# Low parts of selected weight blocks, query-decay products and norm sums issued on VectorE instead of GpSimd

## The chip, the cores and the metric

The kernel runs on one core of a Trainium2 chip. The metric is the device time of one execution in microseconds (us); the time before is the median of three runs. The core has TensorE (matmuls; PE in the profile, its weight loads PEld), VectorE (DVE), ScalarE (ACT), GpSimd (POOL) and the DMA queue of SyncE (SP). Every engine takes its own instructions in the order in which they were put in its queue.

## The reference

One inference step of a two-layer streaming encoder in float32, on 1024 frames of a new stream and 64 frames of a running one; the model width is 1024. Both layers are `x += mixer(rmsnorm(x)); x += conv_ffn(rmsnorm(x))`, and a last RMSNorm follows.

- Layer 0's mixer is multi-scale causal pooling: the mean over a window of 2, 4, 8 or 16 frames less the frame itself, then a 256x256 matrix per group of channels.
- Layer 1's mixer is a gated linear recurrence with 8 heads of dimension 128: `proj = h @ w_in` gives queries, decays f, values and output gates; inside a chunk the products of queries and keys are weighted by the products of the decays between them; a 128x128 state is carried from chunk to chunk; then a norm per head, the gate and `w_out`.
- The ConvFFN is `up = h @ w_up` (2 x 2816 columns), a causal convolution over 3 frames on the gate half, `silu(conv) * val`, and `@ w_down`.

```
def rmsnorm(x, g):    return x * rsqrt(mean(x * x) + EPS) * g
def conv_ffn(h, ...): gate, val = split(h @ w_up); hid = silu(conv3(gate)) * val; return hid @ w_down
```

## The kernel before, in words

Activations lie with the channels on the 128 partitions, 8 tiles of channels, and the 1088 frames in three chunks c of 384, 384 and 320 columns. Each matrix product is made of three TensorE passes in a reduced float32 format (`mm3`, lines 180 to 182): high part of the weight by high part of the data, high by low, low by high. A value a is split into `hi`, a rounding copy on ScalarE, and `lo = a - hi`, a subtraction: `split` (lines 184 to 186) does that for activations and `load_ready` (lines 109 to 130) for weights.

Weights are fetched in blocks of 128x512 by SP into five raw buffers. `load_ready` works a hand-written list (`q_unit`, `q_mix`): as soon as one of 8 slots (12 in the recurrence) is free, the block's `hi` goes to ScalarE (line 128) and its `lo` to GpSimd (line 129). The slot is freed by `drop` when the last matmul with the block has been issued. The list has in this order: the pooling matrices `pw` (4 blocks), layer 0's ConvFFN, the recurrence (phase "g": 64 blocks of `in`, 16 of `out`), layer 1's ConvFFN. In a ConvFFN, j counts 22 tiles of up-projected columns in 11 groups of two. The first group and the last chunk of all groups use plain products (parts a11 to a22 of `up`, which are quarters of the matrix); the other groups use a scheme with seven instead of eight products, whose weights are sums of two raw blocks (made on VectorE, line 152) and whose data are sums of activations (`sums`, lines 423 to 456, on VectorE, made once per layer after the norm). Key `("up", l, j, part)` is such a block, `("upp", ...)` a plain block of the last group, `("dn", l, j, half)` a block of `w_down`.

The RMSNorm (`norm`, lines 353 to 422) has a kind: 0 before layer 0's ConvFFN, 1 before the recurrence, 2 before layer 1's ConvFFN, 3 at the end. It squares the 8 tiles on ScalarE (lines 362 and 365), adds them up in two chains of three additions (line 366: even d and odd d), adds the two (line 373), transposes on TensorE (line 378), makes 1/sqrt in 11 small steps on VectorE (`rstd`, lines 333 to 344), transposes back (line 391), multiplies (line 417) and splits (line 185 `hi`, line 186 `lo`).

The recurrence runs per head h and chunk c: `proj` (queries, decays and so on on TensorE, lines 828 to 867), `core` (lines 870 to 1039), and after two heads `outp`. In `core` line 915 makes `qq = q * f`; then come three levels, and in each VectorE multiplies queries and keys by products of decays (line 936), TensorE makes the scores (line 945, `pl`), and VectorE puts them in place under masks (line 960). A fourth level (lines 969 to 978) and the state follow. Two heads' projections and cores overlap.

The order of TensorE's instructions is written out by the kernel itself (`Task`, `run`): every step gives its own length and the lag until the next step of its task may start, in constants such as `LAT_LEVEL` and `N_RSTD`; the plan does not change with the engine that makes a `lo`. The order on the other engines is set by the compiler's scheduler. VectorE, ScalarE and GpSimd work through their queues in order, so an instruction that waits holds up what is behind it.

Called "turns" here are the stretches in which one stage ends and the next begins: pooling into layer 0's ConvFFN, that into the recurrence, the recurrence into layer 1's ConvFFN.

Of the kernel before, what the change touches and what calls it, by code (L numbers as in the profile page):

```python
# [9 lines left out]
F32 = mybir.dt.float32  # L10
# [4 lines left out]
ALU = mybir.AluOpType  # L15
# [50 lines left out]
def trunk_kernel(ctx: ExitStack, tc: tile.TileContext, xtok, xs_tok, hist_tok, xf, par, gmix, pw, winm, ident_in,  # L66
                 masks_in, w_up, w_dn, w_in, w_out, s0, y_out, npool, nhg, nconv):
    nc = tc.nc
# [30 lines left out]
    def bankB(nm):  # L99
        return pB.tile([P, 512], F32, name=nm, tag="B")  # L100
# [5 lines left out]
    free = [(i, False) for i in range(NR)]  # L106
    extra_w = []

    def load_ready(most=None):

        while queue and (most is None or len(loaded) < most):
            ph, key, make = queue[0]
            own = [p for p in free if p[1]] if ph == "g" and key[:2] not in (("out", H - 2), ("out", H - 1)) else []
            p = own[0] if own else next((p for p in free if not p[1]), None)
            if p is None:
                return
            free.remove(p)
            queue.pop(0)
            places[key] = p
            i, extra = p  # L120
            nm = "_".join(str(k) for k in key)
            if extra:
                hi, lo = (extra_w[i // 2][:, (i % 2 * 2 + b) * HW_:(i % 2 * 2 + b + 1) * HW_] for b in range(2))
            else:
                hi = wp.tile([P, HW_], F32R, name=f"whi{nm}", tag=f"whi{i}", bufs=1)
                lo = wp.tile([P, HW_], F32R, name=f"wlo{nm}", tag=f"wlo{i}", bufs=1)
            src = make(nm)
            nc.scalar.copy(hi, src)  # L128
            nc.gpsimd.tensor_tensor(lo, src, hi.bitcast(F32), op=ALU.subtract)  # L129
            loaded[key] = (hi, lo)  # L130

    def raw_block(nm, src, i):
# [51 lines left out]
    def split(hi, lo, src, lo_eng):  # L184
        nc.scalar.copy(hi, src)  # L185
        lo_eng.tensor_tensor(lo, src, hi.bitcast(F32), op=ALU.subtract)  # L186
# [114 lines left out]
    hn_hi = [hnp.tile([P, ND, NCOL[c]], F32R, name=f"hnhi{c}") for c in range(3)]  # L301
    hn_lo = [hnp.tile([P, ND, NCOL[c]], F32R, name=f"hnlo{c}") for c in range(3)]
# [11 lines left out]
    def piece(what, tag, i, dt):  # L314

        if held.get(tag, (None,))[0] != what:
            held[tag] = what, room(f"{what}{tag}", tag, None, dt)
        return held[tag][1][:, i * NMAX:(i + 1) * NMAX]

    def row(l, c, d):  # L320
        return piece(f"row{l}", *ROWS[c][d], F32)

    def slot(nm, tag, bufs=1, dt=F32, w=SLOT):
        return wk.tile([P, w], dt, name=nm, tag=tag, bufs=bufs)

    def col(base, i):
        return prm[:, base + i:base + i + 1]

    def rstd(ss, nb, nm):

        t = tiny.tile([P, 3, 4], F32, name=f"nt_{nm}", tag="newton")
        m, y, a = (t[:, i, :nb] for i in range(3))
        nc.vector.tensor_scalar(m, ss[0], 1.0 / ss[1], EPS, op0=ALU.mult, op1=ALU.add)
        nc.vector.tensor_scalar(a.bitcast(I32), m.bitcast(I32), 1, None, op0=ALU.logical_shift_right)
        nc.vector.tensor_scalar(y.bitcast(I32), a.bitcast(I32), -1, 0x5F1FFFF9, op0=ALU.mult, op1=ALU.add)

        nc.vector.scalar_tensor_tensor(a, y, -0.703952253, y, op0=ALU.mult, op1=ALU.mult)
        nc.vector.tensor_tensor(a, a, m, op=ALU.mult)
        nc.vector.scalar_tensor_tensor(y, a, 1.68191408, y, op0=ALU.add, op1=ALU.mult)
        nc.vector.tensor_tensor(a, y, y, op=ALU.mult)  # L340
        nc.vector.tensor_tensor(a, a, m, op=ALU.mult)
        nc.vector.tensor_scalar(m, a, 0.375, -1.25, op0=ALU.mult, op1=ALU.add)
        nc.vector.tensor_tensor(a, a, m, op=ALU.mult)
        nc.vector.scalar_tensor_tensor(y, a, 1.875, y, op0=ALU.add, op1=ALU.mult)
        return y

    def blocks(c):
        n = NCOL[c]
        return [(b * P, min(P, n - b * P)) for b in range((n + P - 1) // P)]
# [3 lines left out]
    def norm(c, gbase, nm, kind):  # L353

        final = kind == 3
        n = NCOL[c]
        tags = ("ge", 3, "cv", 3) if kind == 2 else ("e", 2, "v", 2)
        acc = [slot(f"acc{i}_{nm}", *tags[:2]) for i in range(2)]
        for d in range(ND):
            a = acc[d % 2][:, :n]  # L360
            if d < 2:
                nc.scalar.activation(a, x[c][:, d, :], AF.Square)
            else:
                sq = slot(f"sq_{nm}{d}", *tags[2:])
                last = nc.scalar.activation(sq[:, :n], x[c][:, d, :], AF.Square)
                (nc.vector if kind == 0 or final and c == 2 or d % 2 else nc.gpsimd).tensor_tensor(a, a, sq[:, :n], op=ALU.add)
        if final:
            with tc.issue_after(last.ins):
                for d in range(ND):
                    nc.scalar.activation(x[c][:, d, :], x[c][:, d, :], AF.Copy, scale=col(gbase, d))  # L370
        yield 0.0, N_SUM[kind] + N_LATER[0] * (kind == 1 and c > 0)
        a0, acc = acc
        nc.vector.tensor_tensor(acc[:, :n], acc[:, :n], a0[:, :n], op=ALU.add)
        acc = acc[:, :n]
        pt = bankB(f"nps_{nm}")
        blk = blocks(c)
        for i, (o, w) in enumerate(blk):
            nc.tensor.transpose(pt[:w, i * P:(i + 1) * P], acc[:, o:o + w], ident)
        ss = tiny.tile([P, 4], F32, name=f"ss_{nm}", tag="ss")
        full = sum(1 for _, w in blk if w == P)  # L380
        if full < len(blk):
            nc.vector.memset(ss[:, :len(blk)], 1.0)
        nc.vector.tensor_reduce(ss[:, :full], pt[:, :full * P].rearrange("p (b f) -> p b f", f=P), axis=AX.X, op=ALU.add)
        for i, (o, w) in enumerate(blk):
            if w < P:
                nc.vector.tensor_reduce(ss[:w, i:i + 1], pt[:w, i * P:(i + 1) * P], axis=AX.X, op=ALU.add)
        r = rstd((ss[:, :len(blk)], D), len(blk), nm)
        yield 0.11 * len(blk), N_RSTD[kind] + N_LATER[1] * (kind == 1 and c > 0)
        pr = bankB(f"nr_{nm}")
        for i, (o, w) in enumerate(blk):  # L390
            nc.tensor.transpose(pr[:, o:o + w], r[:w, i:i + 1].to_broadcast([w, P]), ident[:w, :w])
        if kind == 0 and c == 1:
            yield 0.0, L_ROWS
        if kind == 0 and c == 0:
            nc.scalar.copy(piece("r0", *T1[6 + c], F32), pr[:, :n])
        if final:
            rs = slot(f"r_{nm}", "cv", 3)
            nc.scalar.copy(rs[:, :n], pr[:, :n])
        while kind == 2 and c < 2 and not last_proj:
            yield 0.0, 0.2  # L400
        for d in range(ND):
            if final:
                on_pool = c < 2 or d in (2, 5)
                eng, r_ = (nc.gpsimd, rs) if on_pool else (nc.vector, pr)
                eng.tensor_tensor(x[c][:, d, :], x[c][:, d, :], r_[:, :n], op=ALU.mult)

                if c < 2 and d % 2 or c == 2 and (d % 2 == 0 or d == ND - 1):
                    d0 = d - (0 < d and (c < 2 or d % 2 == 0))
                    nc.sync.dma_start(y_out[c][:, d0:d + 1, :], x[c][:, d0:d + 1, :])
            else:  # L410
                if kind == 2 and c < 2 or kind == 0 and c == 1:
                    t = row(kind // 2, c, d)
                elif kind == 0 and c < 2:
                    t = slot(f"hn_{nm}{d}", ("hh1", "hl1")[d % 2], 2, F32, NMAX)
                else:
                    t = slot(f"hn_{nm}{d}", "cv", 3)
                last = nc.vector.scalar_tensor_tensor(t[:, :n], x[c][:, d, :], col(gbase, d), pr[:, :n], op0=ALU.mult, op1=ALU.mult)
                split(hn_hi[c][:, d, :], hn_lo[c][:, d, :], t[:, :n], (nc.vector, nc.gpsimd)[d % 2 and kind == 1])
                if d < ND - 1:
                    yield 0.0, N_STEP[kind]  # L420
        return last.ins
# [61 lines left out]
    def token_sums(c):  # L483
# [38 lines left out]
        if c == 0:  # L522
            load_ready(6)
# [346 lines left out]
    def core(h, c, pr, stage):  # L870

        qt, kk, f = (pr[i] for i in ("q", "k", "f"))
        n = NCOL[c]
# [38 lines left out]


        qq, q = qt[:, :n], qt[:, NMAX:NMAX + n]
        nc.gpsimd.tensor_tensor(qq, q, f[:, :n], op=ALU.mult)
        p0 = prod(kk, q, f"pl{nm}_d")
        nc.vector.tensor_tensor(at[:, :so].rearrange("p (b t) -> p b t", t=P), p0[:, :so].rearrange("p (b t) -> p b t", t=P),
                                ident.unsqueeze(1).to_broadcast([P, full, P]), op=ALU.mult)
# [6 lines left out]
        for lev in range(3):  # L925
# [26 lines left out]
            for i, ps in enumerate(pls):  # L952
                r, num = blk[2 * i][1], min(2, nb - 2 * i)
                dst = at[:r, 2 * i * P:2 * i * P + num * r].rearrange("p (b m w) -> p b m w", b=num, w=4 * hh)
                src = ps[:r, :num * 3 * r // 2].rearrange("p (b e m w) -> p b e m w", b=num, e=2, w=3 * hh)
# [224 lines left out]
```

## Time and profile before

| | us |
|---|---|
| median of 3 runs (2372.25 to 2373.45) | 2372.37 |
| the profiled execution | 2377.06 |
| its span, first to last instruction | 2375.2 |
| TensorE busy | 2284.7 (96%) |
| VectorE busy | 1613.8 (68%) |
| GpSimd busy | 1003.0 (42%) |
| ScalarE busy | 904.3 (38%) |
| granted TensorE clock, mean | 0.981 |

The span is the time from the first to the last instruction of the profiled execution. "Busy" is the union of an engine's instructions; 38111 instructions were recorded, 13830 of them matmuls. The granted clock is a share of TensorE's full rate of 2.4 GHz; at its lower level it runs at 1.2 GHz, and that level shows as 0.5.

### The profile page before, as it was taken

What the parts mean: (1) busy time and instruction counts of PE and PEld (TensorE: products, weight loads), DVE (VectorE), ACT (ScalarE), POOL (GpSimd) and SP (SyncE); (2) the same over time, 40 slices, a digit from 0 to 9 for tenths busy, and PEclk for the clock granted to TensorE, in tenths of its full rate; (3) what the DMA queues carried; (4) which work ended last, traced back from release to release, by engine and by line L of the source; (5) the groups of instructions that cost most, each with busy time, mean ns of one, the idle gap of its engine ahead of it and who ended that gap; (6) DMA issues with size and microseconds to landing.
All of it is one profiled execution on the core that took longest, in us unless ns stands there. A gap on an engine that the chain in (4) does not pass through costs nothing. (4 is left out here: it accounts for less than half of the span.)

```text
span 2375.2 us, 38111 instructions
## 1 busy us (share of the span) xinstructions
PE 2284.7 (96%) x13830; PEld 2231.3 (94%) x13830; DVE 1613.8 (68%) x3728; ACT 904.3 (38%) x1965; POOL 1003.0 (42%) x1054
## 2 busy tenths in 40 slices
PE   9889999999999989999999999889999999999996
PEld 8889999999999989999999999878999999999996
DVE  6786656566666688767667767778766666666567
ACT  5444333334433353323323322345333333443335
POOL 1155554556655562112112211224454555564555
PEclk8999999999999999999999999989999999999998
DMA  7123333333433321001011000102343334433431
GB/s 233 49 81 116 125 121 120 123 125 129 138 116 125 124 69 36 26 18 54 26 35 40 32 26 22 36 25 76 111 130 116 125 119 134 134 124 117 129 120 76
DMA packets 118099, 218.70 MB, mean 92 GB/s; under 512 B 13436, under 2 KB 17404, under 8 KB 117528
## 3 DMA queue, kind: packets, MB, share of 16 engines
q1 hardware_dynamic: 117822, 216.15, 28.0%
q8 instruction: 109, 1.79, 0.3%
q14 instruction: 78, 0.64, 0.1%
q10 hardware_dynamic: 90, 0.12, 0.0%
HBM read 210.51 MB, written 5.72 MB: 91 GB/s over the span
## 5 line engine op out<-in xcount | busy, mean ns | idle before, releaser
L129 POOL TENSOR_TENSOR wloup_a<-rawup_a,whiup_a 128x512 fp32r<-128x512 f32 x368 | 513.1, 1411 | 568.1 <-ACT whiup_a L128 534.4
L128 ACT CAST whiup_a<-rawup_a 128x512 fp32r<-128x512 f32 x368 | 224.2, 617 | 573.8 <-PE dn L181 397.4
L152 DVE TENSOR_TENSOR rawup_a<-rawup_a,rawup_a 128x512 f32<-128x512 f32 x200 | 186.6, 933 | 286.4 <-DMA rawup_a<-w_up_in 261.4
L180 PE MATMUL dn<-hh,whidn 128*128 128x384 f32 (+1 forms) x1056 | 351.5, 333 | 11.5 <-DVE x L757 8.0
L181 PE MATMUL dn<-hl,whidn 128*128 128x384 f32 (+1 forms) x1056 | 348.7, 330 | 0.7 <-DVE hl L186 0.7
L182 PE MATMUL dn<-hh,wlodn 128*128 128x384 f32 (+1 forms) x1056 | 348.9, 330 | 0.0
L757 DVE TENSOR_TENSOR x<-x,dn 128x384 f32<-128x384 f32 (+1 forms) x528 | 262.3, 528 | 97.1 <-PE dn L182 95.5
L180 PEld LDWEIGHTS dn<-hh,whidn 128*128 128x128 f32 x1056 | 200.2, 190 | 18.0 <-DVE x L757 13.4
L181 PEld LDWEIGHTS dn<-hl,whidn 128*128 128x128 f32 x1056 | 200.1, 190 | 1.3 <-DVE hl L186 1.3
L182 PEld LDWEIGHTS dn<-hh,wlodn 128*128 128x128 f32 x1056 | 200.1, 189 | 0.0
L180 PE MATMUL pj<-hnhi,whiin 128*128 128x384 f32 (+1 forms) x528 | 185.0, 350 | 1.1 <-ACT hnhi L185 1.1
L181 PE MATMUL pj<-hnlo,whiin 128*128 128x384 f32 (+1 forms) x528 | 173.0, 328 | 2.4 <-POOL hnlo L186 2.4
L182 PE MATMUL pj<-hnhi,wloin 128*128 128x384 f32 (+1 forms) x528 | 173.2, 328 | 0.0
L630 DVE SCALAR_TENSOR_TENSOR cv<-ge,prm,cv 128x322 f32<-128x322 f32 (+1 forms) x132 | 132.1, 1002 | 48.2 <-ACT cv L629 42.0
L129 POOL TENSOR_TENSOR wlodn<-rawdn,whidn 128x512 fp32r<-128x512 f32 x88 | 119.0, 1354 | 100.9 <-ACT whidn L128 76.8
L960 DVE COPY_PREDICATED at<-masks,pl 128x64 f32<-128x64 uint8 (+7 forms) x432 | 117.0, 293 | 50.5 <-PE pl L945 48.8
L632 ACT ACTIVATE cv<-cv 128x322 f32<-128x322 f32 (+1 forms) x132 | 67.2, 509 | 161.3 <-DVE cv L631 160.9
L180 PE MATMUL pv<-hnhi,whiup_a 128*128 128x320 f32 (+1 forms) x384 | 122.1, 318 | 0.0
L180 PE MATMUL pg<-hnhi,whiup_a 128*128 128x320 f32 (+1 forms) x384 | 122.1, 318 | 0.0
L182 PE MATMUL pg<-hnhi,wloup_a 128*128 128x320 f32 (+1 forms) x384 | 121.7, 317 | 0.0
L182 PE MATMUL pv<-hnhi,wloup_a 128*128 128x320 f32 (+1 forms) x384 | 121.5, 317 | 0.0
L181 PE MATMUL pg<-hnlo,whiup_a 128*128 128x320 f32 (+1 forms) x384 | 121.5, 316 | 0.0
(1234 smaller groups left out, 6199.0 us busy)
## 6 DMA issues: line engine op xcount, KB each, us to landing
rawup_a<-w_up_in SPq DMA_DIRECT2D x568, 256.0 KB, 2.8
rawdn<-w_dn_in SPq DMA_DIRECT2D x88, 256.0 KB, 3.1
rawin<-w_in_in SPq DMA_DIRECT2D x64, 256.0 KB, 2.6
rawupp_a<-w_up_in SPq DMA_DIRECT2D x16, 256.0 KB, 2.7
rawout<-w_out_in SPq DMA_DIRECT2D x16, 256.0 KB, 2.7
xt<-xtok_in SPq DMA_DIRECT2D x7, 448.0 KB, 6.7
x<-xf_in SPq DMA_DIRECT2D x2, 1536.0 KB, 8.7
y_out<-x SPq DMA_DIRECT2D x8, 384.0 KB, 2.3
```

Source lines behind the costliest of these rows:

```text
L128: nc.scalar.copy(hi, src)
L129: nc.gpsimd.tensor_tensor(lo, src, hi.bitcast(F32), op=ALU.subtract)
L152: nc.vector.tensor_tensor(t[0], t[0], t[1], op=bs[2])
L180: nc.tensor.matmul(ps, w[0][:, wsl], a_hi, start=first, stop=False, skip_group_check=more)
L181: nc.tensor.matmul(ps, w[0][:, wsl], a_lo, start=False, stop=False, skip_group_check=more)
L182: nc.tensor.matmul(ps, w[1][:, wsl], a_hi, start=False, stop=last, skip_group_check=more)
L630: nc.vector.scalar_tensor_tensor(t[:, :wd], ge[:, 0:wd], prm[:, cw[0]:cw[0] + 1], t[:, :wd], op0=ALU.mult, op1=ALU.add)
L632: nc.scalar.activation(t[:, :wd], t[:, :wd], AF.Silu)
L757: nc.vector.tensor_tensor(x[c][:, d, :], x[c][:, d, :], pd[:, :n], op=ALU.add)
L960: nc.vector.copy_predicated(dst[:, :, :, d * hh:], mk, a)
```

## The change

The `lo` of a weight block is made on VectorE for all blocks of the recurrence, for `pw`, for `up` with j below 4 and for `dn` with j below 2 of both layers; all other blocks stay on GpSimd. By the list these are 4 `pw`, 80 blocks of the recurrence, and 30 for each layer (8 plain blocks for j = 0 and 1, 9 each for j = 2 and 3, 4 of `dn`): 144. In `norm`, the additions of even d move from GpSimd to VectorE for kinds 1 and 2 (kind 0 had them there, kind 3 is as before). The `lo` of odd d in kind 1 moves to VectorE. In `core` the product `qq` moves to VectorE (24 instructions). What is computed, the transfers, TensorE's and ScalarE's instructions stay as they are.

```diff
+    def lo_engine(ph, key):
+        return nc.vector if ph == "g" or key[0] == "pw" or key[0] in ("up", "dn") and key[2] < (4, 2)[key[0] == "dn"] else nc.gpsimd
...
             nc.scalar.copy(hi, src)
-            nc.gpsimd.tensor_tensor(lo, src, hi.bitcast(F32), op=ALU.subtract)
+            lo_engine(ph, key).tensor_tensor(lo, src, hi.bitcast(F32), op=ALU.subtract)
...
-                (nc.vector if kind == 0 or final and c == 2 or d % 2 else nc.gpsimd).tensor_tensor(a, a, sq[:, :n], op=ALU.add)
+                (nc.vector if kind < 3 or c == 2 or d % 2 else nc.gpsimd).tensor_tensor(a, a, sq[:, :n], op=ALU.add)
...
-                split(hn_hi[c][:, d, :], hn_lo[c][:, d, :], t[:, :n], (nc.vector, nc.gpsimd)[d % 2 and kind == 1])
+                split(hn_hi[c][:, d, :], hn_lo[c][:, d, :], t[:, :n], nc.vector)
...
-        nc.gpsimd.tensor_tensor(qq, q, f[:, :n], op=ALU.mult)
+        nc.vector.tensor_tensor(qq, q, f[:, :n], op=ALU.mult)
```

## Rows read from the trace of the kernel before

**Rows 1.** The page, its first lines: span, and busy time of each engine.
```profile
span 2375.2 us, 38111 instructions
...
PE 2284.7 (96%) x13830; PEld 2231.3 (94%) x13830; DVE 1613.8 (68%) x3728; ACT 904.3 (38%) x1965; POOL 1003.0 (42%) x1054
```

**Rows 2.** Busy time by stretch; after the engines the granted clock, DMA share, GB/s.
```profile
0.00:126.00 126.00, 111.22 (x690) 107.88 (x691) 90.08 (x237) 64.80 (x133) 18.06 (x28) 0.89 0.42 133
126.00:170.00 44.00, 38.60 (x240) 37.44 (x239) 40.80 (x66) 22.90 (x49) 31.42 (x26) 1.00 0.27 86
170.00:836.00 666.00, 659.16 (x3960) 655.31 (x3959) 424.49 (x674) 252.61 (x492) 361.68 (x386) 1.00 0.38 124
836.00:895.00 59.00, 49.55 (x276) 47.06 (x275) 52.30 (x114) 31.44 (x64) 37.69 (x33) 0.91 0.18 60
...
945.00:1515.00 570.00, 562.92 (x3550) 538.07 (x3549) 389.47 (x1456) 169.84 (x485) 103.08 (x102) 1.00 0.10 32
1515.00:1592.00 77.00, 61.08 (x315) 55.54 (x314) 58.85 (x174) 31.27 (x75) 15.25 (x16) 0.82 0.06 19
1592.00:1670.00 78.00, 71.15 (x413) 67.98 (x412) 66.07 (x118) 34.36 (x72) 33.75 (x39) 0.96 0.25 82
```

**Rows 3.** Waits of PE in 0:126, 836:895, 1515:1592: us in total, times, longest.
```profile
PE nps_f L378 <- DVE acc_f L373: 6.1, 2, 3.9
...
PE pj L181 <- POOL hnlo L186: 2.4, 1, 2.4
...
PE pl L945 <- DVE q__16127 L936: 7.3, 2, 3.9
```

**Rows 4.** Timeline near 1091 us, POOL, DVE and PE: start, length, instruction.
```profile
1091.00 1.26 POOL L129 TENSOR_TENSOR wloin<-rawin,whiin 128x512 fp32r<-128x512 f32 x1 [9.78 <-ACT whiin L128]
...
1091.08 1.29 DVE L936 TENSOR_TENSOR q__11445<-q__11445,tp 128x96 f32<-128x96 f32 x1
...
1092.52 0.40 PE L945 MATMUL pl<-q__11445,k__11634 128*128 128x192 f32 x1 [1.35 <-DVE q__11445 L936]
```

**Rows 5.** Timeline near 1026 us, DVE and PE: a level of the recurrence.
```profile
1025.98 0.24 DVE L936 TENSOR_TENSOR q__10771<-q__10771,tp 128x80 f32<-128x80 f32 x1
...
1027.15 0.33 PE L945 MATMUL pl<-q__10771,k__10842 128*128 128x192 f32 x1
```

**Rows 6.** Timeline of DVE near 1646 us, with GpSimd idle.
```profile
1645.60 0.68 DVE L152 TENSOR_TENSOR rawup_a<-rawup_a,rawup_a 128x512 f32<-128x512 f32 x1
1646.20 0.55 DVE L186 TENSOR_TENSOR mix1w<-sum,mix1w 128x384 fp32r<-128x384 f32 x1
```

**Rows 7.** Instructions of line 129 alone by stretch: POOL's busy time (count), granted clock.
```profile
836.00:895.00 59.00, 18.34 (x13) 0.91 0.18 60
945.00:1515.00 570.00, 78.86 (x61) 1.00 0.10 32
...
1620.00:1645.00 25.00, 12.75 (x8) 0.88 0.26 85
```

**Rows 8.** Groups of DVE in 1620:1642: count, busy us, mean ns of one.
```profile
L186 DVE TENSOR_TENSOR hnlo<-sum,hnhi 128x384 fp32r<-128x384 f32 x7 | 7.0, 1014 | 0.0
L437 DVE TENSOR_TENSOR sum<-row1w 128x384 f32<-128x384 f32 x6 | 4.2, 732 | 0.0
L631 DVE SCALAR_TENSOR_TENSOR cv<-ge,prm,cv 128x322 f32<-128x322 f32 x2 | 2.1, 1059 | 0.0
L437 DVE TENSOR_TENSOR sum<-row1w,row1f 128x384 f32<-128x384 f32 x1 | 1.6, 1641 | 0.0
L437 DVE TENSOR_TENSOR sum<-row1q,row1w 128x384 f32<-128x384 f32 x1 | 1.6, 1614 | 0.0
```

**Rows 9.** Timeline of DVE in 1524:1531: three steps of a 1/sqrt.
```profile
1524.84 0.88 DVE L337 SCALAR_TENSOR_TENSOR nt_g<-nt_g 128x3 f32<-128x3 f32 x1
1525.76 0.16 DVE L338 TENSOR_TENSOR nt_g<-nt_g 128x3 f32<-128x3 f32 x1
...
1529.45 1.22 DVE L342 TENSOR_SCALAR nt_g<-nt_g 128x3 f32<-128x3 f32 x1
```

## Prediction, made before the change was run

> **What bounds the kernel now.** I read the page first: TensorE is busy for 2284.7 of 2375.2 us [rows 1]. The change leaves its instructions alone, so it can give back only idle time of TensorE, 90.5 us in all, and what TensorE loses where its clock is halved. The second view, busy time by stretch, says where that is [rows 2]. In 170:836, the body of the first ConvFFN, TensorE idles for 6.8 us of 666; nothing is to be had there, though GpSimd is busy for 361.68 us. The turns are different. Idle of TensorE: 14.8 us in 0:126, 5.4 in 126:170, 9.4 in 836:895, 15.9 in 1515:1592, 6.9 in 1592:1670; the recurrence, 945:1515, has 7.1. In three of these the granted clock is under 1: 0.91, 0.82 and 0.96, worth 0.09 x 59 + 0.18 x 77 + 0.04 x 78 = 22.3 us of full rate. VectorE is nearly full in the turns (40.80 of 44, 52.30 of 59, 66.07 of 78 us) and at 68% in the recurrence (389.47 of 570).
>
> The third view, who TensorE waits for, names VectorE nearly everywhere and GpSimd once: a norm's sum, 6.1 us in the first stretch; the low part of a normalised tile on GpSimd, 2.4 us at the turn into the recurrence; the factor products of the last core, 7.3 us [rows 3]. So VectorE's speed in the turns is the question, and the fourth view shows what slows it: at 1091.08 a product of 96 columns takes 1.29 us, and it ends with a weight's low part that GpSimd began at 1091.00; TensorE has by then waited 1.35 us [rows 4]. A product of 80 columns with GpSimd idle takes 0.24 us [rows 5]. A VectorE instruction with two SBUF inputs is therefore held by GpSimd's to its end, about 1.05 us here. Rows 5 also show the reserve of a level of the recurrence: the product ends at 1026.22, TensorE uses it at 1027.15, 0.93 us later.
>
> **Prices.** A low part on VectorE: no subtraction of that shape is there, but line 152 adds two 128x512 tiles in SBUF in 0.68 us, and its successor starts 0.60 us after it [rows 6]; I take 0.60, with 0.68 as the upper end. The 128x384 operations (norm additions, low parts of tiles, qq) are like line 186 in the same rows: 0.55 us, 0.47 where they stand back to back, by the same 0.08 of overlap. On GpSimd a weight's low part costs 78.86 / 61 = 1.29 us in the recurrence and 12.75 / 8 = 1.59 in a turn [rows 7]. VectorE gets 144 x 0.60 = 86 us, 18 norm additions, 12 low parts and 24 qq at 0.47 = 25 us: 111 us on an engine that idles for 2375.2 - 1613.8 = 761. The sum alone decides nothing; each stretch does.
>
> **Turn into layer 0 (0:126), +1.** Freeing the four `pw` blocks loads four `up` blocks just ahead of the norm sum for which TensorE waits [rows 3]: up to 4 x 0.60 = 2.4 us more in front of it. Two earlier pairs of low parts may hold VectorE less than before, by 4 x (1.05 - 0.60). Ends -1.8 and +2.4; I take +1.
>
> **Second halves of both ConvFFN turns (126:170 and 1592:1670), -2.7 each.** In 1620:1642 VectorE works without a gap on `sums`, and GpSimd makes 8 low parts [rows 7], all of j under 4 or of `dn` under 2, so all move. What the port takes from VectorE there is the excess over an undisturbed length (0.55 us for 384 columns, some 0.54 for the convolution): 7 x 0.46 + 6 x 0.18 + 2 x 0.52 + 1.09 + 1.06 = 7.5 us [rows 8]. Their own work is 8 x 0.60 = 4.8. VectorE is done 2.7 us sooner, and TensorE, which waits for its results, idles for 6.9 us in this turn, so the gain gets through. Layer 0 has the same sequence with 40.80 of 44 us busy and 5.4 us of idle [rows 2]; I take the same. Ends for each: the idle, -5.4 and -6.9, and 0.
>
> Here a rule speaks against the change. The Trainium skill (Trace analysis, Optimizing Scalar/DVE Operations) says that work may be taken off a saturated VectorE, to GpSimd even, and adds that between these two it might not help, since they share a read port. By its first half 4.8 us would be lost in each of these turns; by the rows the port takes 7.5 us.
>
> **Turn into the recurrence (836:895), -2.4.** To VectorE go 12 low parts (the 13th of [rows 7] is of the last group and stays), 8 low parts of tiles and 9 norm additions: 7.2 + 3.8 + 4.2 = 15.2 us, where VectorE has 6.7 us of idle and GpSimd's 37.69 us of holding go away almost wholly. I take these as even, since the blocked time there is spread over many small steps. What is left is the wait of 2.4 us for a tile's low part, which stands in GpSimd's queue behind weights at 1.4 us each (18.34 / 13); on VectorE it takes 0.55. Ends: all the idle, -9.4, and the work that finds no idle, 15.2 - 6.7 = +8.5.
>
> **Recurrence (945:1515), -1.5.** 61 low parts [rows 7] and 21 qq: 36.6 + 9.9 us of new work beside 180 us of idle. A low part now waits in VectorE's queue for ScalarE's high part, with the factor products (line 936) and the masks (line 960) behind it, and TensorE's scores wait for those. Where it is in front it holds the chain 0.60 us, not 1.05; a wait such as that of 1.35 us becomes 0.90. A third of 7.1 us is 2.4; I keep 1.5, as some levels have less reserve than 0.93. Ends -7.1 and the first rival's price.
>
> **Turn out of the recurrence (1515:1592), -1.7.** In 1524:1531 five of the eleven steps of a 1/sqrt take 0.88 to 1.22 us, the first and last of which are shown, instead of 0.16 [rows 9]: between 5 x 0.72 = 3.6 and 5 x 1.06 = 5.3 us more; I take 4.3. Behind them stand the products for which TensorE waits 7.3 us in two waits [rows 3]. GpSimd holds them with three norm additions and two low parts, whose own work is 3 x 0.47 + 2 x 0.60 = 2.6. Ends -7.3 and +2.6.
>
> **Clock, -3.** Parts two, three and five give back 6.8 of 32.2 us of idle in the three stretches with a lowered clock, 21%; of 22.3 us that is 4.7. A stretch at 1.2 GHz that ends in a wait gives nothing back, so 3. Ends 0 and -12.
>
> **The rest at nothing.** SP issues a transfer when a raw buffer is freed, which the low part does; a shorter one frees it earlier, and in the bodies, where GpSimd keeps its blocks, the transfers hide under TensorE. ScalarE's squares in the norms wait for VectorE's additions instead of GpSimd's. What covers a late low part is that a block is loaded when a slot is freed and used only after the blocks ahead of it in the list; without that cover TensorE would wait those 0.60 us, or a pair's 1.20, for every such block.
>
> Sum: +1 - 2.7 - 2.7 - 2.4 - 1.5 - 1.7 - 3 = -13.0. The profiled execution took 2377.06 us, 1.9 more than its span, and would take 2364; the median stands 4.7 us below it, at 2372.37, and goes to **2359.4**.
>
> **Rivals.** (1) *The recurrence's VectorE chain becomes late, slower.* `drop` frees both halves of a matrix at once, so low parts come in pairs in some 30 levels. A pair is 1.20 us, and if it waits 0.6 for ScalarE (one such operation's length), 1.80 against a reserve of 0.93: 0.87 x 30 = 26 us more, 14.6 after the 11.5 of the other parts, 2387. It decides from about 13 late levels on (11.5 / 0.87). For it: rows 5 show little reserve, and queues are in order. Against: VectorE idles for a third of the stage, and holds of 1.05 us go. Chance 0.12.
> (2) *A full engine gets fuller, slower:* the blocks' own work adds, and little comes back, since GpSimd's remaining operations hold VectorE as before. +2.4 + 4.8 + 4.8 + 2.6 - 2.4 - 1.5 = +10.7: 2383. The first half of the Trainium skill's rule above (Trace analysis, Optimizing Scalar/DVE Operations) would have it so. Against it stands the excess in [rows 8]. Chance 0.05.
> (3) *The port's time comes back as own work:* only the 2.4 us of GpSimd's late tile goes, the first turn's +1 stays: 2371. For it: 111 us are added, and work and holds are near each other in every part. Chance 0.15.
> (4) *The waits fall under what halves the clock:* half of the 22.3 us returns, and the turn out of the recurrence gives its whole 7.3: -10 - 11 - 5.6 = 2346. Against: most waits shrink by a third only. Chance 0.18.
> That the moves aren't made is excluded: each is a named engine in the diff.
>
> **Numbers.** Forecast 0.50, its own range 2350 to 2367. What a measurement can tell from no change is 0.2%, 4.7 us. Faster by more: forecast and rival 4, 0.68; within: rival 3, 0.15; slower: rivals 1 and 2, 0.17. The range takes in rivals 3 and 4 and some of the lesser loss: 2344 to 2377.
>
> **What would show it.** In the trace after: the step at 1.29 us [rows 4] back near 0.25, GpSimd nearly idle in the recurrence; line 129 on VectorE at 0.6 to 0.7 us; PE's wait for GpSimd's tile gone; the 1/sqrt steps near 0.16 in the turn out of the recurrence and its wait of 7.3 us at 5 to 6; idle in 1592:1670 some 4 us. Wrong it would be if waits for line 936 in 945:1515 grew beyond 7 us, if line 129 on VectorE showed long waits for ScalarE, or if the turns kept their idle with VectorE's own work in the place of the holds.

## The result, and the profile after

The changed kernel takes 2341.64 us (median of four runs, 2340.37 to 2346.42) against 2372.85 for the kernel before beside it: a ratio of 0.987, 95% interval 0.9856 to 0.9884, that is 31.2 us less. Forecast were 13.0 less, to 2359.4, in a range from 2344 to 2377: the direction and the cause were right, the forecast gain was less than half of the measured one, and the time lies 2.4 us under the range. The fourth rival, 2346, came nearest.

The first lines of the page after, span and busy time of each engine:

```profile
span 2339.5 us, 38021 instructions
...
PE 2269.2 (97%) x13830; PEld 2219.9 (95%) x13830; DVE 1621.5 (69%) x3926; ACT 904.5 (39%) x1965; POOL 755.1 (32%) x856
```

The profiled execution of the changed kernel took 2341.33 us. Beside [rows 1] the span is 35.7 us shorter (4.5 more than the medians differ by; the execution that was profiled before lay 4.7 above its median). Two things make up the 35.7. TensorE idles 70.3 us instead of 90.5, 20.2 less. And it is busy for 15.5 us less with the same 13830 matmuls; its mean granted clock rose from 0.981 to 0.988, so fewer of them ran at the lower level. The forecast held 10.0 us for idle time and 3 for the clock. VectorE took on 198 instructions and is busy for only 7.7 us more: the holds that went were nearly as long as the work that came.

Busy time by stretch after, with borders at the same matmuls as in [rows 2]; the columns are as there:

```profile
0.00:117.70 117.70, 103.91 (x690) 99.74 (x691) 92.19 (x249) 64.72 (x133) 2.90 (x16) 0.97 0.45 143
117.70:158.10 40.40, 37.73 (x240) 37.41 (x239) 39.27 (x79) 23.68 (x50) 13.81 (x13) 1.00 0.32 98
158.10:823.30 665.20, 659.00 (x3960) 655.33 (x3959) 426.11 (x684) 252.45 (x491) 348.29 (x376) 1.00 0.39 124
823.30:881.00 57.70, 48.76 (x276) 47.34 (x275) 53.14 (x143) 30.61 (x64) 2.10 (x3) 0.91 0.19 61
931.00:1494.40 563.40, 562.47 (x3550) 538.07 (x3549) 395.10 (x1541) 170.19 (x485) 2.02 (x20) 1.00 0.10 32
1494.40:1561.20 66.80, 55.78 (x315) 51.21 (x314) 55.96 (x181) 31.31 (x77) 0.38 (x3) 0.90 0.06 19
1561.20:1635.60 74.40, 71.16 (x412) 68.33 (x411) 63.23 (x139) 34.21 (x72) 8.52 (x20) 0.95 0.28 89
```

Both kernels issue the same matmuls in the same order, so the time at which each comes can be compared. The stretches gave back, in us, by the borders of [rows 2]: the first 8.4; 126:170 3.6, and 2.3 more up to 200; the body of layer 0 took back 1.4; 836:895 1.3 (3.6 up to 861 us, of which 2.3 went again behind it); the recurrence 6.6; 1515:1592 10.3; 1592:1670 3.5, and 0.7 up to 1700; after that 0.7. In the recurrence TensorE's idle time fell from 7.1 to 0.9 us.

The same level of the recurrence as in [rows 4], on DVE and PE, some 14 us earlier in the span (line 132 is the low part, line 939 the factor products, line 948 the scores):

```profile
1077.29 0.26 DVE L939 TENSOR_TENSOR q__11445<-q__11445,tp 128x96 f32<-128x96 f32 x1
...
1077.60 0.71 DVE L132 TENSOR_TENSOR wloin<-rawin,whiin 128x512 fp32r<-128x512 f32 x1
...
1077.70 1.05 PE L948 MATMUL pl<-q__11445,k__11634 128*128 128x192 f32 x5 [0.31 <-DVE q__11445 L939]
```

The product that took 1.29 us takes 0.26, TensorE waits 0.31 instead of 1.35, and the low part stands behind the product in VectorE's queue, not in front of it. The steps of the 1/sqrt of [rows 9] (lines 337 and 342, now 340 and 345) likewise:

```profile
1504.58 0.15 DVE L340 SCALAR_TENSOR_TENSOR nt_g<-nt_g 128x3 f32<-128x3 f32 x1
...
1507.28 0.16 DVE L345 TENSOR_SCALAR nt_g<-nt_g 128x3 f32<-128x3 f32 x1
```

Who PE waited for after, in 0:117.7 and in 1494:1561.2 (us in total, times, longest):

```profile
PE pg L185 <- DVE wloup_a L132: 3.4, 1, 3.4
PE pd L568 <- DVE wr L547: 1.6, 2, 1.3
...
PE pl L948 <- DVE at L963: 4.2, 1, 4.2
PE pl L975 <- DVE k__16198 L939: 1.4, 1, 1.4
```

The wait of 3.4 us for a low part is new, the change made it. The first product's wait, 3.9 us before, is 1.3, and the 7.3 us for the last core's products in [rows 3] are 4.2, now for the masks behind them.

A second new wait is in the turn into the recurrence, of 3.5 us; timeline of DVE in 846:858.5 and of PE in 857:858.4:

```profile
855.38 1.89 DVE L132 TENSOR_TENSOR wx<-rawin,wx 128x512 fp32r<-128x512 f32 x3
857.18 1.67 DVE L760 TENSOR_TENSOR x<-x,dn 128x320 f32<-128x320 f32 x4
...
857.71 0.64 PE L183 MATMUL dn<-hh,whidn 128*128 128x320 f32 x1 [3.48 <-DVE x L760]
```

The wait of 2.4 us for GpSimd's tile [rows 3] is gone, but TensorE now waits for VectorE's additions (line 760), and three low parts of the recurrence stand right in front of them. They are not the whole of it: in the trace of the kernel called "the rest alone" below, where no weight's low part moved, the longest wait for line 760 in this turn is still 2.2 us.

### The profile page after: what moved, and what is told of

Read it like the earlier page. It is cut to its first block, busy times and chain, and to the rows that moved or that the text cites. A ratio compares the mean times of both kernels' runs of the same rounds, so it can differ in the third digit from the quotient of the medians.

```text
span 2339.5 us, 38021 instructions
## 1 busy us (share of the span) xinstructions
PE 2269.2 (97%) x13830; PEld 2219.9 (95%) x13830; DVE 1621.5 (69%) x3926; ACT 904.5 (39%) x1965; POOL 755.1 (32%) x856
## 4 chain that ended last, share of the span: by engine, by line
PE 86%; DVE 7%; DMA 2%; ACT 2%; POOL 2%; issue 1%; SPq 0%; DVEq 0%; POOLq 0%; ACTq 0%
PE dn L183 7%; PE dn L184 6%; PE dn L185 6%; PE pj L183 6%; PE pj L185 5%; PE pj L184 5%; PE pz L184 3%; PE pz L185 3%; PE pz L183 3%; PE pl L948 3%; PE pv L183 2%; PE pg L183 2%; PE pv L184 2%; PE pv L185 2%; PE pg L185 2%; PE pg L184 2%
## 5 line engine op out<-in xcount | busy, mean ns | idle before, releaser
L132 POOL TENSOR_TENSOR wloup_a<-rawup_a,whiup_a 128x512 fp32r<-128x512 f32 x316 | 439.6, 1408 | 458.8 <-ACT whiup_a L131 428.7
L132 POOL TENSOR_TENSOR wlodn<-rawdn,whidn 128x512 fp32r<-128x512 f32 x80 | 106.2, 1329 | 88.3 <-ACT whidn L131 83.1
```

The lines of the kernel that those rows point to most:

```text
L132: lo_engine(ph, key).tensor_tensor(lo, src, hi.bitcast(F32), op=ALU.subtract)
```

## The experiments

**One part of the change at a time.** Four kernels made from the one before, each with one part:

```diff
+    def lo_engine(ph, key):
+        return nc.vector if key[0] == "pw" else nc.gpsimd
...
+        return nc.vector if ph == "g" else nc.gpsimd
...
+        return nc.vector if key[0] in ("up", "dn") and key[2] < (4, 2)[key[0] == "dn"] else nc.gpsimd
```

The three conditions belong to the first three; the fourth has the changed lines of `norm` and of `qq` alone.

> Only the low parts of the four pw blocks are moved to VectorE. Theory (holds and clock): GpSimd's low part at 12.5 us no longer holds the step of the 1/sqrt that took 1.22 us, TensorE's first wait of 3.9 us falls to some 1.3, the stretch at 1.2 GHz of 17 us that follows it goes, and nearly all of what the changed kernel is ahead at 30 us (8 us) is here: 2365 us. Rival (the clock of the start differs from one execution to the next, whatever the kernel): the wait gets shorter by 1 to 3 us but the half-rate stretch stays or comes and goes: 2370 to 2373.

> Only the low parts of the recurrence's 80 blocks are moved. Theory (holds): the waits of 1.3 to 1.5 us for line 936 shrink to a third, the stretch 895 to 1515 gives 5 to 6.5 us as in the changed kernel, the turn into it 1: 2366 us. Rival (GpSimd was only slow or late with the blocks TensorE needs): the recurrence's blocks are fetched long before their use, so nothing moves: 2372. Second rival (my own forecast's size): 1.5 us, 2371.

> Only the low parts of up (j under 4) and dn (j under 2) are moved, 60 blocks. Theory (holds): the second halves of both ConvFFN turns give 5.8 and 3.4 us, the turn out of the recurrence a part (two low parts among five holds), 2 to 4: 2360 us. Rival (VectorE is full there, own work eats it): 2370.

> No weight's low part is moved; only the norm additions of kinds 1 and 2, the tiles' low parts of kind 1, and qq. Theory (holds): three of the five holds of the 1/sqrt steps at 1524 to 1531 go, and with them a part of the 10 us which the changed kernel gains in 1515 to 1592; the wait of 2.4 us for GpSimd's tile at 861 goes: 2365 us. Rival (the low parts of weights hold VectorE in any case): 2371.

| kernel | median us | ratio to before | interval |
|---|---|---|---|
| pw alone | 2372.2 | 0.9984 | 0.9972 to 0.9995 |
| recurrence alone | 2367.41 | 0.9958 | 0.9942 to 0.9974 |
| turns alone | 2362.45 | 0.9943 | 0.9922 to 0.9963 |
| the rest alone | 2369.58 | 0.9971 | 0.9959 to 0.9982 |

On this chip the kernel before had a median of 2375.9; the expectations were reckoned from 2372.85, so their ratios are compared: 0.9967, 0.9971, 0.9946 and 0.9967 by the theories. The recurrence, the turns and the rest agree with them within their intervals; the pw part gave about its rival's (0.9988 to 1), not its theory's. The four parts sum to 0.0016 + 0.0042 + 0.0057 + 0.0029 = 1.44%, the whole change gave 1.30%: within their intervals the gains add. In the trace of the recurrence part alone the recurrence gained 6.5 of the 6.6 us that it gained in the whole, so the moved low parts did that by themselves. The turns part gained 5.8 us in 126:200, 6.0 in 1515:1592 and 3.7 in 1592:1700, the rest 5.6 in 1543:1592. The pw part was worth less than its theory, and its trace shows why: TensorE's first wait fell to 1.35 us, but from 16 to 30 us its clock was still at the lower level.

**Reading, or only running.** What is it in GpSimd's instructions that VectorE suffers from? The changed kernel, with a GpSimd instruction on the dead raw block in each of the 144 places, once one that reads and writes it, once one that only writes it:

```diff
             lo_engine(ph, key).tensor_tensor(lo, src, hi.bitcast(F32), op=ALU.subtract)
+            if lo_engine(ph, key) is nc.vector:
+                nc.gpsimd.tensor_tensor(src, src, src, op=ALU.subtract)
```

In the second kernel the last line is `nc.gpsimd.memset(src, 0.0)`.

> The changed kernel, and for each of the 144 blocks whose low part VectorE now makes, GpSimd subtracts the block from itself in place once its low part is taken (a result that nothing reads): VectorE keeps the new work, GpSimd reads and writes the same 128x512 numbers for about 1.2 us as before the change. Theory, that while a GpSimd instruction reads SBUF a VectorE instruction with two inputs stands still: nearly the time of before comes back, 2365 to 2376, and the length of VectorE's instructions in the second halves of the turns and in the recurrence, over what the same instructions take undisturbed, is 40 us of it or more in the recurrence (12 after the change, 41 before). Rival, that the low parts were only late on GpSimd's queue and that the hold cost nothing: 2342 to 2347.

> The changed kernel, and for each of the 144 moved blocks GpSimd fills the dead raw block with zeros once its low part is taken: a write with no input, in the same places of the order, and the raw block comes free as late as with the subtraction. Theory, that it is GpSimd's reads against VectorE's that hold: 2341 to 2346. Rival, that any GpSimd instruction on SBUF holds VectorE while it runs: the time goes up in proportion to its length, to 2350 or more. If this one and the subtraction both come to 2360 or more, it is the raw blocks' later release that costs, not the hold.

Reading: 2391.66, ratio 1.0074 (1.0046 to 1.0102). Writing: 2347.61, ratio 0.9884 (0.9861 to 0.9907), 1.6 us above the bounds of its theory and under those of its rival. The first is even slower than the kernel before, and than its theory said; VectorE now has the holds and the work. Busy time of the factor products alone (line 936 before, 939 after, 941 in these two) in the recurrence, in this order before, after, reading, writing; the columns are the window, its length, DVE's busy time (count), granted clock, DMA share, GB/s:

```profile
945.00:1515.00 570.00, 132.33 (x432) 1.00 0.10 32
```
```profile
931.00:1494.40 563.40, 116.97 (x432) 1.00 0.10 32
```
```profile
953.10:1521.90 568.80, 131.62 (x433) 1.00 0.10 31
```
```profile
937.60:1500.90 563.30, 117.02 (x432) 1.00 0.10 32
```

The same products (433 within the borders of the reading kernel) take 132 us when GpSimd reads and 117 when it is idle or only writes. The time of the recurrence goes with them: TensorE idles for 7.1, 0.9, 4.5 and 0.9 us in these four stretches. GpSimd's own 61 instructions there were busy for 66.62 us in the reading kernel and 32.11 in the writing one, about half; a hold by writing in the same measure would show as some 7 of the 15 us, and 0.05 show. Instruction by instruction it is as clear: 35 products of the reading kernel begin while one of the 144 added instructions runs, take 0.77 us on average, and all end 0.11 to 0.22 us after it; in the writing kernel 38 begin so and take 0.26 on average. Of the small steps of a 1/sqrt, 8 begin so in the reading kernel and all take 0.8 us or more, 10 in the writing kernel and all take 0.15 to 0.16. A pair from the reading kernel's timeline, POOL and DVE:

```profile
950.04 1.04 POOL L134 TENSOR_TENSOR rawout<-rawout 128x512 f32<-128x512 f32 x1 [2.80 <-issue]
...
950.12 1.13 DVE L941 TENSOR_TENSOR q__10033<-q__10033,f__10105 128x80 f32<-128x80 f32 x1
```

A product of 80 columns, 0.24 us by [rows 5], ends after GpSimd's instruction has ended. The theory stands, and the rival, that low parts were merely late on GpSimd, is out: they are on VectorE in both kernels. A later release of the raw blocks isn't it either: in the recurrence SP waits as long for GpSimd's instructions on them in both, 398 and 387 us. The Trainium skill (SBUF — State Buffer, Who interferes with whom) says just this, that a VectorE instruction with two SBUF inputs contends with GpSimd instructions that read SBUF and not with those that only write; the four rows agree. The writing kernel's median lies 5.8 us over that of the changed kernel beside it (next section). That is not in the recurrence (6.5 us gained there, as after): of the 7.9 us between the two traces 6.3 were lost in the first 32 us, to the clock.

**The start, and the clock there.** The first 11 us hold 76 fill matmuls, which multiply a constant tile and whose result nothing reads; then comes the first product (line 565 before, 568 after, weights `wr`). The expectations call `pw` "the first product's weights"; they are those of the product after it. What a low part of `pw` on GpSimd holds is a step of the 1/sqrt that `wr` waits for, before the change, POOL and DVE:

```profile
12.47 1.26 POOL L129 TENSOR_TENSOR wlopw<-rawpw,whipw 128x512 fp32r<-128x512 f32 x1 [11.54 <-ACT whipw L128]
12.54 1.22 DVE L339 SCALAR_TENSOR_TENSOR nt_p<-nt_p 128x4 f32<-128x4 f32 x1
```

The changed kernel again, and with the pw parts back on GpSimd:

```diff
-        return nc.vector if ph == "g" or key[0] == "pw" or key[0] in ("up", "dn") and key[2] < (4, 2)[key[0] == "dn"] else nc.gpsimd
+        return nc.vector if ph == "g" or key[0] in ("up", "dn") and key[2] < (4, 2)[key[0] == "dn"] else nc.gpsimd
```

> The changed kernel once more, on this chip, for a second trace. If the half-rate stretch of 17 us at the start of before was an accident of one execution, this trace may show such a stretch and a time some 6 to 8 us above 2342; if the low parts of the first product's weights on VectorE take it away, there is none in the first 60 us again, and 2341 to 2344.

> The changed kernel with only the four low parts of the first product's weights back on GpSimd. Theory, that they are worth what the first 60 us gained (8 to 9 us at the same matmul in the two traces): the first wait is 3 to 4 us again, a half-rate stretch of 10 us or more follows it, 2347 to 2351. Rival, that they are worth only the wait of 2.6 us and the rest was the clock of one execution: 2342 to 2345.

Again: 2341.77, ratio 0.9863 (0.9837 to 0.9889). Without pw: 2344.92, 0.9881 (0.9854 to 0.9907), 3.2 us more and inside the rival's bounds. Yet the trace showed what the theory wanted. Busy time from 14 to 32 us, before, again, without pw (columns as in [rows 2]):

```profile
14.00:32.00 18.00, 16.75 (x75) 16.76 (x76) 8.67 (x25) 8.57 (x17) 4.14 (x4) 0.53 0.57 189
```
```profile
14.00:32.00 18.00, 17.52 (x127) 17.36 (x128) 15.47 (x39) 14.89 (x30) 0.00 (x0) 1.00 0.92 318
```
```profile
14.00:32.00 18.00, 16.95 (x82) 16.78 (x83) 9.32 (x25) 9.54 (x18) 3.84 (x3) 0.62 0.57 189
```

In the first and third stretch TensorE's granted clock is at its lower level, 1.2 GHz, for 17.1 and 13.7 us. That costs 6 to 8 us. Such a stretch of 14 to 17 us stood in all six traces with pw on GpSimd, and in five of the ten of kernels with pw on VectorE and the same fill, among them the kernel with the pw part alone and the writing kernel. In those ten the 76 fill matmuls ahead of the first product last 11.2 to 11.6 us where the stretch is absent and 10.2 to 11.1 where it follows, and TensorE's wait for the first product is 1.3 to 1.7 us where it is absent and 1.4 to 2.5 where it follows; with pw on GpSimd the wait is 2.6 to 3.9, and there the stretch also followed a fill of 11.46 us. So it is partly the chance of an execution, and a single trace can't price that step.

**What the change itself made late.** The new wait of 3.4 us is for a low part that stands behind 10 us of norm work in VectorE's queue. That one block, of each layer, back on GpSimd:

```diff
-        return nc.vector if ph == "g" or key[0] == "pw" or key[0] in ("up", "dn") and key[2] < (4, 2)[key[0] == "dn"] else nc.gpsimd
+        return nc.vector if ph == "g" or key[0] == "pw" or key[0] in ("up", "dn") and key[2] < (4, 2)[key[0] == "dn"] and key[2:] != (1, "a11") else nc.gpsimd
```

> The changed kernel with one low part in each layer, that of the block a11 of up 1, back on GpSimd (2 of the 144). On VectorE it stands in the queue behind 10 us of norms and TensorE waits 3.4 us for it at 92 us and 1.3 us at 1561. Theory (what the change cost, it cost by VectorE's order, and one held instruction of 1.2 us costs less): both waits shrink to under 1 us, 2336 to 2341. Rival, that the matmuls then wait as long for the next thing on VectorE (the norm's steps, 0.7 us later each): 2341 to 2344.

2346.65, ratio 0.9882 (0.9853 to 0.9911): no gain, and above the bounds of both expectations. PE's waits in 90:112, after and then in this kernel:

```profile
PE pg L185 <- DVE wloup_a L132: 3.4, 1, 3.4
PE nps_f L381 <- DVE acc_f L376: 1.5, 1, 1.5
```
```profile
PE nps_f L381 <- DVE acc_f L376: 3.9, 1, 3.9
PE pg L185 <- DVE wloup_a L132: 1.3, 1, 1.3
```

The rival's mechanism was right: VectorE's chain of the norm sets this place, and TensorE waits for it one step later.

**The end.** After, from 2306 us, GpSimd multiplies the last norm's tiles while VectorE has a chain of small steps, POOL and DVE:

```profile
2306.90 8.45 POOL L408 TENSOR_TENSOR x<-x,r_o 128x384 f32<-128x384 f32 x8
```
```profile
2307.21 0.97 DVE L344 TENSOR_TENSOR nt_o<-nt_o 128x3 f32<-128x3 f32 x1
2308.22 0.93 DVE L345 TENSOR_SCALAR nt_o<-nt_o 128x3 f32<-128x3 f32 x1
```

The edit makes these multiplications wait until the last hidden block is issued; the second kernel joins it with the edit before:

```diff
+        while final and c < 2 and not last_hid:
+            yield 0.0, 0.2
         for d in range(ND):
             if final:
...
             hidden(j, jj, c, cv, pv, hid)
+            if l and x and jj:
+                last_hid.append(True)
```

> The changed kernel with the last norm's 16 multiplications on GpSimd issued after the last hidden block instead of before it. The nine VectorE instructions on the chain from 2306 to 2314 us took 9.4 us, undisturbed by other rows some 3.5. Theory (GpSimd's reads hold them): they take 3 to 4 us, the last hidden block comes 4 to 6 us earlier, and of it 2 to 4 us are left at the end, since GpSimd then ends later and holds the sums of the last norm: 2337 to 2340. Rival: GpSimd's 17 us of multiplications and their output transfers, started 8 us later, become the end: 2344 to 2350.

> The edits of the first-block run and of the tail run together. Theory: their gains add, 2332 to 2338, under both kernels. Rival: either edit's gain is taken back by the clock or the order, 2340 to 2344.

2344.32, ratio 0.9875 (0.9844 to 0.9906), and 2344.1, ratio 0.9868 (0.9836 to 0.99): neither can be told from the changed kernel, and both medians lie above the bounds of their theories. In the trace of the tail edit some 2 us were gained from 2300 us on, as expected; its first 32 us lost 7.5 to the clock. Only two of the four last steps of the 1/sqrt came back to 0.16: an order of issue binds GpSimd's queue to nothing on VectorE's, and two multiplications still ran beside them. The hold was lessened, not removed.

**All low parts on VectorE.** The other 412 too:

```diff
     def lo_engine(ph, key):
-        return nc.vector if ph == "g" or key[0] == "pw" or key[0] in ("up", "dn") and key[2] < (4, 2)[key[0] == "dn"] else nc.gpsimd
+        return nc.vector
```

> The changed kernel with every low part of the weights on VectorE, the 412 of the steady ConvFFN stages too (0.68 us each, 280 us more VectorE work, less some 110 us of holds). Theory (a hold costs only where VectorE is the chain that TensorE waits for; in the steady stages TensorE was busy 99%): no gain there, 2339 to 2345. Rival 1 (holds cost everywhere): 2325 to 2335. Rival 2 (VectorE's queue makes low parts late, as at 92 us): 2350 or more.

2329.07, ratio 0.9818 (0.9784 to 0.9853). The theory fell: there was a gain, 14.8 us in the trace against that of the changed kernel. By the borders of [rows 2] 8.0 us of it came between 300 and 836 us, 2.4 in 836:895 and 4.8 in the other body, from 1700 to 2290. Of the first body I had written that TensorE is busy 99% and nothing is to be had. The changed kernel's timeline of DVE and PE at 434 us shows what was missed:

```profile
434.21 0.69 DVE L155 TENSOR_TENSOR rawup_a<-rawup_a,rawup_a 128x512 f32<-128x512 f32 x1 [3.24 <-DMA rawup_a<-w_up_in]
434.81 1.41 DVE L760 TENSOR_TENSOR x<-x,dn 128x384 f32<-128x384 f32 x3
...
435.42 0.42 PE L183 MATMUL dn<-hh,whidn 128*128 128x320 f32 x1 [1.54 <-DVE x L760]
```

VectorE waits in order for a transfer to add two raw blocks, and the additions that TensorE needs stand behind it. Waits in 158:815 after (DVE, PE, and the DMA queue of SP):

```profile
DVE rawup_a L155 <- DMA rawup_a<-w_up_in: 122.7, 52, 4.0
PE dn L183 <- DVE x L760: 3.8, 4, 1.5
SPq L137 <- POOL wloup_a L132: 211.7, 110, 7.2
```

and with all low parts on VectorE, where PE's wait for line 760 is gone:

```profile
DVE rawup_a L155 <- DMA rawup_a<-w_up_in: 42.1, 45, 2.4
SPq L137 <- DVE wloup_a L132: 268.1, 157, 7.8
```

SP can't fetch into a raw buffer until the low part of the block in it is made. Compared at the same matmuls, the low parts in this stretch end 1.0 us sooner on average and SP issues the transfers of `w_up` 1.1 us sooner. VectorE waits 80 us less for them, though that isn't all earlier transfers: it is also busy for 65 us more there, and work that stands in the place of a wait shortens it. Held instructions get shorter too: the sums of two raw blocks that VectorE makes (line 155) take 0.70 us on average instead of 0.94. So rival 1's time came, if not by holds alone; how much each of these gave wasn't separated.

**Together, and the start once more.** Three kernels from this one: with the tail's edit; with pw back on GpSimd; and with a longer fill ahead of the first product:

```diff
-        fill(T_FILL)
+        fill(T_FILL + 1.6)
```

> All low parts on VectorE and the last norm's 16 GpSimd multiplications after the last hidden block. Theory: the tail's edit gave 2 us in its trace from 2300 us on, so 2 us under the all-VectorE kernel's 2329: 2325 to 2328. Rival: with no low parts left on GpSimd its multiplications run in an idle stretch anyway and the edit gives nothing: 2328 to 2331.

> All low parts on VectorE but the four of the first product's weights, which are on GpSimd as before the change. Theory (they take away the half-rate stretch at the start in some executions): the stretch is there in the trace, most times lie in the upper of two groups some 6 us apart, median 2331 to 2335. Rival (the stretch comes or goes by itself): 2327 to 2330.

> All low parts on VectorE, and 7 more fill matmuls (45 for 38) ahead of the first product, so that TensorE's wait of 1.3 to 2.5 us at 12 us is filled with work. Theory (the wait brings the half-rate stretch of 14 to 17 us that follows in some executions): no such stretch, all times in the lower group, median 2325 to 2328. Rival (the stretch has another cause): times as spread as without, 2328 to 2331.

| kernel | median us | ratio to before | interval |
|---|---|---|---|
| all, and the tail's edit | 2333.47 | 0.9821 | 0.9803 to 0.9839 |
| all, pw on GpSimd | 2334.13 | 0.9821 | 0.9803 to 0.9839 |
| all, longer fill | 2327.27 | 0.979 | 0.977 to 0.9809 |

The tail's edit gives nothing that can be measured; its median lies above the bounds of both expectations, and its trace, beside that of all low parts, lost 7.4 us in the first 32 us and gained 1.0 after 2290. Without pw on VectorE the low clock was there again, as its theory had it, and the median came out in its bounds, but the kernel with the tail's edit had both pw on VectorE and the low clock. The longer fill had no such stretch in its trace and the lowest median of all kernels, with times from 2323.51 to 2329.83. Fill and first product on PE, with the tail's edit and then with the longer fill:

```profile
1.05 10.23 PE L262 MATMUL fill<-warm 128*128 128x128 f32 x76 [1.05 <-DVE pss L516]
13.71 0.69 PE L571 MATMUL pd<-wr,xt 96*128 96x96 f32 x4 [2.42 <-DVE wr L550]
```
```profile
1.05 12.37 PE L262 MATMUL fill<-warm 128*128 128x128 f32 x90 [1.05 <-DVE pss L513]
13.66 0.69 PE L568 MATMUL pd<-wr,xt 96*128 96x96 f32 x4 [0.23 <-DVE wr L547]
```

The wait of 2.42 us is 0.23, and the first product starts no later. This kernel is 2.1% under the one before and about 0.8% under the changed one by the ratios (0.979 and 0.987). That the fill takes away the low clock is not shown: it rests on one trace and on times that lie within 6.3 us, the trace of all low parts with the shorter fill had no such stretch either, and against that kernel (0.9818) the intervals still overlap.

## Why the prediction was right and wrong

**Right: the cause.** It rested on one rule read from [rows 4, 8, 9], that a VectorE instruction with two SBUF inputs, and a small step as well, stands while GpSimd reads. The reading and the writing kernel show it for both. Rivals 1, 2 and 3 are out: the gain was far over rival 3's, waits for the factor products in the recurrence fell to 0.3 us, no late level appeared. The rule from the Trainium skill that I set against the change (Perfetto Trace Analysis, Optimizing Scalar/DVE Operations: a saturated VectorE may hand work to GpSimd) would have made rival 2 come true, slower by 10.7; here taking work back from GpSimd gave 31. The warning in the sentence after it, that the two share a read port, agrees with the runs.

**Right in size:** the second halves of the ConvFFN turns, -2.7 each, gave 3.6 and 3.5 within their stretches; idle in 1592:1670 was to be some 4 us and was 3.2. The turn into the recurrence, -2.4, gave 1.3, about half: the wait for GpSimd's tile went, but the new one for line 760 came, which the prediction had nowhere. The first stretch's price of up to 2.4 us for low parts was right in size by luck, not in its order: it was to be a longer wait for the norm's sum, but that wait, 3.9 us before, is 1.5, and the first low part behind the norm is late by 3.4. Between 66 and 110 us 2.1 us were lost.

**Wrong: the step "Clock, -3".** This is the largest miss. I counted "three of these" stretches with a clock under 1, though [rows 2] shows 0.89 for the first one as well: 0.11 x 126 = 13.9 us that the sum never held. By the rows of both kernels the lost full-rate time in the four stretches was 13.9 + 5.3 + 13.9 + 3.1 = 36.2 and is 3.5 + 5.2 + 6.7 + 3.7 = 19.1: 17.1 us came back, 10.4 in the first stretch and 7.2 in 1515:1592. Of this, what fell into matmuls shows in TensorE's busy time: 15.5 us less in all, 7.3 of them in the first stretch. These, and 1.0 us of idle time, turn the step "0:126, +1" into a gain of 8.4. Part of the first stretch's gain was luck, as the start's runs show. By the ratios of three pairs with and without pw on VectorE (0.9984 to 1, 0.9863 to 0.9881, 0.9818 to 0.9821) those parts are worth 1 to 4 us, with intervals as wide as that; how much of the rest a new execution would show stays open.

**Wrong: the step "Recurrence, -1.5".** I let a low part stand in front of the chain for 0.60 us and kept a third of the idle. It stands behind the product instead (1077.60 after 1077.29), the waits of 1.3 us became 0.3, 6.2 of the 7.1 us of idle came back, and the stretch got 6.6 us shorter; the recurrence part alone gave 6.5.

**Wrong: the step "Turn out of the recurrence, -1.7".** The excess of the 1/sqrt went as reckoned, 4.3 us; but I took 2.6 off for own work on the path, most of which found room, and idle fell by 4.9 us, from 15.9 to 11.0. The other 5.3 us of this stretch are busy time, matmuls no longer at half rate: the fourth rival's mechanism. Its number came near for another reason in part: in the three stretches that it counted 6.7 of the 22.3 us came back, not half, and it had nothing for the first stretch and 1.5 for the recurrence.

**Wrong, though it cost the forecast nothing: "the rest at nothing".** The bodies' transfers were said to hide under TensorE. For the change, which left those blocks alone, that was nearly so: layer 0's body took back 1.4 us. The kernel with all low parts on VectorE shows that they did not hide wholly, and TensorE's waits for line 757 (now 760) were there before the change as well, 4.3 us in 158:836.

## What to carry to other kernels

Where two engines hold each other, price a move by the holds that end, from the rows of held instructions, and then ask what is late behind them: with 198 more instructions VectorE was busy for 0.5% longer, and the kernel ran 1.3% shorter. Take the granted clock of every stretch into the sum, and ask of a gap at the start or in a turn not only how long it is but whether a low clock follows it. A body in which TensorE is busy 99% can still give: look for an in-order queue that waits for a transfer, and for what frees that transfer's buffer.

## What the runs showed of the hardware that was not expected

- The VectorE instructions that were held ended with the GpSimd instruction beside them, whatever their own size: steps on 128x3 elements took 0.91 to 0.97 us each beside GpSimd's multiplications of 1.05 us, and 0.16 alone.
- The same 76 fill matmuls lasted 10.2 to 11.6 us from one execution to the next, and the granted clock of the 14 to 17 us after them was at one level or the other: at the lower in all ten traces whose fill took up to 11.14 us, and in one of the six with a fill of 11.2 or more. That is worth 6 to 8 us of 2340. Which comes first, and what a move on VectorE does to it, stays open. It is enough to hide every edit of this study that is worth 2 us.
- GpSimd instructions that only write held the factor products not at all: 117.02 us beside 116.97.
